# A gap of 192 bytes below the left-hand activation tiles of a diffusion block kernel

## Chip, cores and metric

One core of one Trainium2 chip runs the kernel. The metric is the device time of one execution in microseconds (us); the median of three runs before the change is 1629.53 us (1629.22 to 1630.85).

## What is computed

One block of a diffusion backbone over 256 latent tokens and 256 context tokens, width 2048, all in fp32. Cut to what matters:

```python
mod = silu(c) @ w_ada + b_ada                       # shifts, scales, gates for both sub-layers
h_lat, h_ctx = modulate(rmsnorm(x)), modulate(rmsnorm(ctx))
dq, dk, dv, cq, ckv, kr, ga, gb = split(h @ w_in)   # 8000 columns
o_da  = differential attention(dq, dk, dv)          # 8 heads
o_mla = latent attention(rmsnorm(cq) @ w_uq, rmsnorm(ckv) @ w_ukv, kr)
x = x + g1 * ((sigmoid(ga) * (rmsnorm(o_da) @ w_o_da) + sigmoid(gb) * (o_mla @ w_o_mla)) @ w_out)
h2 = modulate(rmsnorm(x))
x = x + g2 * ((silu(h2 @ w_ffn_gate) * (h2 @ w_ffn_up)) @ w_ffn_down)   # hidden width 5632
return rmsnorm(x)
```

## The kernel before

**Matrix products.** Each fp32 operand is held as a high part rounded to fp32r and a low part (the rest), and each product takes three matmuls: high x high, high x low, low x high. Weights arrive by 512 KB transfers from SyncE's queue into `raw` (five buffers, `load_w`), ScalarE rounds them into `wh` (three buffers, L140) and VectorE subtracts to make `wl` (three buffers, L141); the activation pairs (`hl`, `hc`, `oTa`, `oTb`, `cqn`, `ckvn`, `mT`, `h2`, `hid`) stay in SBUF. `group_t` computes 512 output columns for 256 tokens: the stationary operand is a 128x128 block of weights, the moving operand a 128x256 slice of the activations. One `group_t` over all 16 slices of the inner width is 8 units of 24 matmuls, 192 in all (over 8 slices, 4 units and 96). `group_b` turns it round: activations are stationary and the weights move (256 columns in `dv`, 512 in `down`). Each matmul has a weight load of its own, so every matmul reads one slice as moving operand while the next stationary block is being read. `Acc.mm` (L125, L127) issues them all.

**Stages.** Modulation and the first projections; four rounds of differential attention (`dk`, `dq`, `dv` from `hl`, `hc`); latent attention (`cq`, then `kn`, `mv`, `qn`, `qr` from `ckvn`, `cqn`); four rounds of `ga`, `gb` (from `hl`) and two `yab` (from `oTa`, `oTb`); `wo` (from `mT`); eleven rounds of `gate` and `up` (from `h2`, L889 to L901); four rounds of `down` (from `hid`). Beside them a generator (`gemv`, L452) streams parts of `w_ada` through the same `raw` buffers and sums them on VectorE (`gacc`, L461): a call of `tick` loads one 512 KB piece. In the FFN the `gate` rounds 3 to 6 have such a tick with each unit; `up` rounds have none. The order of TensorE's work is that of the program, and SyncE's queue issues the loads in program order as buffers come free.

**Where tiles lie.** Pools are two stacks in each partition's 224 KiB: `const`, `stream` (wl, wh, raw) and then all other pools opened without a side grow upwards from the left; pools with `side="right"` grow down from the top end. Every slice that a matmul reads starts a multiple of 512 bytes into its tile. The compiled program of before places them so (bytes within a partition):

| tiles | side | start | start mod 256 | mod 512 |
|---|---|---|---|---|
| wl, wh, three each | left | 25,120 to 45,600 in steps of 4,096 | 32 | 32 |
| ckvn (high, low) | left | 70,176 and 74,272 | 32 | 32 |
| h2 | left | 86,560 and 102,944 | 32 | 32 |
| oTa | left | 110,368 and 118,560 | 32 | 288 |
| oTb | left | 126,752 and 134,944 | 32 | 288 |
| cqn | left | 143,136 and 147,232 | 32 | 288 |
| hc, later mT | right | 163,808 and 180,192 | 224 | 480 |
| hl | right | 196,576 and 212,960 | 224 | 480 |
| hid | right | 130,528 and 175,584 | 224 | 480 |

In the differential attention the topmost left tile (`dvl`) ends at 163,616, and `hc` begins at 163,808.

Of the kernel before, what the change touches and what calls it, by code (L numbers as in the profile page):

```python
# [11 lines left out]
F32 = mybir.dt.float32  # L12
# [6 lines left out]
P = 128  # L19
# [49 lines left out]
def kernel(  # L69
# [11 lines left out]
    def pool(name, bufs=1, space=None, side=None):  # L81
        st = ExitStack()
        kw = {}
        if space is not None:
            kw["space"] = space
        if side is not None:
            kw["side"] = side
        pl = st.enter_context(tc.tile_pool(name=name, bufs=bufs, reuse_waits="tile", **kw))
        return pl, st.close
# [2 lines left out]
    ctx.callback(_c0)  # L92
    stream, _c1 = pool("stream")
    ctx.callback(_c1)
    pacc, _c2 = pool("pacc", space=PSUM)
    ctx.callback(_c2)

# [872 lines left out]
```

## Time and profile before

| | |
|---|---|
| median of three runs | 1629.53 us |
| profiled execution | 1625.1 us |
| its span, first to last instruction | 1623.3 us |
| TensorE busy | 1574.0 us (97%) |
| VectorE, ScalarE busy | 1018.1 us (63%), 736.6 us (45%) |
| read from HBM | 352.37 MB, 218 GB/s over the span |

The span is 1.8 us shorter than the profiled execution's own time. Busy time of TensorE counts each matmul from its start to a modelled end, and neighbours overlap; how fast matmuls follow one another is read from the length of an unbroken stretch divided by the matmuls in it. The views used are the page's tables, the chain of work that ended last, sums over windows of time, and groups by line.

### The profile page before, as it was taken

What the parts mean: (1) busy time and instruction counts of PE and PEld (TensorE: products, weight loads), DVE (VectorE), ACT (ScalarE), POOL (GpSimd) and SP (SyncE); (2) the same over time, 40 slices, a digit from 0 to 9 for tenths busy, and PEclk for the clock granted to TensorE, in tenths of its full rate; (3) what the DMA queues carried; (4) which work ended last, traced back from release to release, by engine and by line L of the source; (5) the groups of instructions that cost most, each with busy time, mean ns of one, the idle gap of its engine ahead of it and who ended that gap; (6) DMA issues with size and microseconds to landing.
All of it is one profiled execution on the core that took longest, in us unless ns stands there. A gap on an engine that the chain in (4) does not pass through costs nothing.

```text
span 1623.3 us, 28926 instructions
## 1 busy us (share of the span) xinstructions
PE 1574.0 (97%) x11936; PEld 1467.9 (90%) x11936; DVE 1018.1 (63%) x1356; ACT 736.6 (45%) x1033; POOL 16.1 (1%) x14
## 2 busy tenths in 40 slices
PE   4999999999999999899999999999999999999997
PEld 1778899999899999899999999999999999888886
DVE  6437888677875867677767476766444544444454
ACT  4325455546774434344346434444444344344343
POOL 0000000000000000000000000000000000011010
PEclk9999999999999999999999999999999999999999
DMA  9995754453347889888985677887666666656563
GB/s 330 353 354 170 220 157 144 130 170 101 96 130 235 296 285 305 278 282 279 309 275 169 187 265 263 267 279 246 184 184 185 185 184 199 201 191 189 193 194 117
DMA packets 197075, 356.35 MB, mean 220 GB/s; under 512 B 11984, under 2 KB 71632, under 8 KB 196688
## 3 DMA queue, kind: packets, MB, share of 16 engines
q1 hardware_dynamic: 196080, 351.58, 68.0%
q10 hardware_dynamic: 864, 2.93, 0.6%
q8 instruction: 93, 1.52, 0.4%
q14 instruction: 38, 0.31, 0.1%
HBM read 352.37 MB, written 2.10 MB: 218 GB/s over the span
## 4 chain that ended last, share of the span: by engine, by line
PE 75%; DMA 8%; DVE 4%; issue 1%; ACT 1%; DVEq 0%; POOLq 0%; POOL 0%; ACTq 0%; SPq 0%
PE gate L127 15%; PE up L127 15%; PE down L127 15%; DMA raw<-in_w_ada_dram 6%; PE dv L127 5%; PE yab L127 3%; PE ga L127 3%; PE gb L127 3%; PE dk L127 3%; PE wo L127 2%; PE dq L127 2%; DVE wl L141 1%; PE cq L127 1%; DVE gacc L461 1%; PE pt L601 1%
## 5 line engine op out<-in xcount | busy, mean ns | idle before, releaser
L141 DVE TENSOR_TENSOR wl<-raw,wh 128x1024 fp32r<-128x1024 f32 x452 | 550.3, 1223 | 375.5 <-ACT wh L140 352.7
L140 ACT CAST wh<-raw 128x1024 fp32r<-128x1024 f32 x452 | 474.2, 1050 | 628.3 <-PE down L127 137.1
L461 DVE SCALAR_TENSOR_TENSOR gacc<-raw,cols,gacc 128x1024 f32<-128x1024 f32 x120 | 153.9, 1283 | 97.3 <-DMA raw<-in_w_ada_dram 97.1
L127 PE MATMUL up<-h,wh 128*128 128x256 f32 x1386 | 183.8, 283 | 0.0
L127 PE MATMUL gate<-h,wh 128*128 128x256 f32 x1386 | 183.7, 283 | 0.0
L127 PEld LDWEIGHTS gate<-h,wh 128*128 128x128 f32 x1386 | 174.3, 192 | 0.4 <-DVE h L855 0.2
L127 PE MATMUL down<-wh,hid 128*128 128x512 f32 x696 | 174.5, 391 | 0.0
L127 PEld LDWEIGHTS up<-h,wh 128*128 128x128 f32 x1386 | 174.2, 192 | 0.0
L127 PEld LDWEIGHTS down<-wh,hid 128*128 128x128 f32 x696 | 130.8, 188 | 28.8
L127 PE MATMUL up<-h,wl 128*128 128x256 f32 x704 | 100.6, 283 | 0.0
L127 PE MATMUL gate<-h,wl 128*128 128x256 f32 x704 | 100.6, 283 | 0.0
L127 PE MATMUL down<-wl,hid 128*128 128x512 f32 x352 | 95.6, 392 | 0.0
L127 PEld LDWEIGHTS gate<-h,wl 128*128 128x128 f32 x704 | 91.6, 192 | 0.0
L127 PEld LDWEIGHTS up<-h,wl 128*128 128x128 f32 x704 | 91.6, 192 | 0.0
L127 PEld LDWEIGHTS down<-wl,hid 128*128 128x128 f32 x352 | 66.1, 188 | 14.1
L127 PE MATMUL ga<-hl,wh 128*128 128x256 f32 x504 | 65.4, 278 | 0.0
L127 PE MATMUL gb<-hl,wh 128*128 128x256 f32 x504 | 64.0, 277 | 0.0
L127 PE MATMUL wo<-mT,wh 128*128 128x256 f32 x504 | 63.7, 277 | 0.0
L127 PEld LDWEIGHTS ga<-hl,wh 128*128 128x128 f32 x504 | 61.1, 188 | 0.1
L127 PEld LDWEIGHTS gb<-hl,wh 128*128 128x128 f32 x504 | 60.6, 188 | 0.0
L127 PEld LDWEIGHTS wo<-mT,wh 128*128 128x128 f32 x504 | 60.1, 188 | 0.4 <-issue 0.4
L363 PE MATMUL pgb<-sraw,c 128*32 128x512 f32 x244 | 37.2, 607 | 20.5 <-DMA sraw<-in_w_ada_dram 20.5
(335 smaller groups left out, 2320.3 us busy)
## 6 DMA issues: line engine op xcount, KB each, us to landing
raw<-in_w_ada_dram SPq DMA_DIRECT2D x128, 512.0 KB, 4.7
raw<-in_w_in_dram SPq DMA_DIRECT2D x120, 512.0 KB, 4.8
raw<-in_w_ffn_gate_dram SPq DMA_DIRECT2D x88, 512.0 KB, 4.4
raw<-in_w_ffn_up_dram SPq DMA_DIRECT2D x88, 512.0 KB, 4.2
raw<-in_w_ffn_down_dram SPq DMA_DIRECT2D x88, 512.0 KB, 3.8
sraw<-in_w_ada_dram SPq DMA_DIRECT2D x122, 256.0 KB, 6.6
raw<-in_w_out_dram SPq DMA_DIRECT2D x32, 512.0 KB, 6.0
raw<-in_w_o_da_dram SPq DMA_DIRECT2D x16, 512.0 KB, 5.5
```

The lines of the kernel that those rows point to most:

```text
L127: nc.tensor.matmul(region, lhsT, rhs, start=False, stop=last, skip_group_check=key != self.lead)
L140: nc.scalar.copy(h, v)
L141: nc.vector.tensor_sub(l, v, h.bitcast(F32))
L363: nc.tensor.matmul(pgb[32 * j : 32 * j + 32, :], c32[:, kt, :], vs[kt], start=kt < 4, stop=kt >= 12, tile_position=(0, 32 * j))
L461: nc.vector.scalar_tensor_tensor(a, raw, cols[:, kt : kt + 1], a, op0=ALU.mult, op1=ALU.add)
L601: nc.tensor.transpose(pt[:, j * P : (j + 1) * P], a[:, j * P : (j + 1) * P], ident)
```

## The change

It opens one more pool on the left, after `stream` and before all the others, with one tile of 48 floats (192 bytes) per partition that nothing writes or reads. Every left-hand pool opened later starts 192 bytes higher; `const`, `stream` and the right-hand pools stay where they are. No instruction is added or taken away.

```diff
     stream, _c1 = pool("stream")
     ctx.callback(_c1)
+
+    apart, _c3 = pool("apart")
+    ctx.callback(_c3)
+    apart.tile([P, 48], F32, name="gap")
     pacc, _c2 = pool("pacc", space=PSUM)
     ctx.callback(_c2)
```

So `ckvn` and `h2` start at 224 mod 256 (224 mod 512), and `oTa`, `oTb` and `cqn` at 224 mod 256 (480 mod 512).

## Rows read from the trace of the kernel before

**Rows 1.** The page: busy time by engine, and the granted TensorE clock in 40 slices
```profile
PE 1574.0 (97%) x11936; PEld 1467.9 (90%) x11936; DVE 1018.1 (63%) x1356; ACT 736.6 (45%) x1033; POOL 16.1 (1%) x14
...
PEclk9999999999999999999999999999999999999999
```
**Rows 2.** The chain that ended last, four stretches: start us, us, what, matmuls
```profile
277.68 21.19 PE dv L127 x187
...
549.01 21.19 PE ga L127 x187
...
570.77 21.19 PE gb L127 x187
...
843.92 10.90 PE wo L127 x96
```
**Rows 3.** The same chain in the FFN
```profile
887.10 22.44 PE up L127 x187
...
910.14 22.44 PE gate L127 x187
...
1372.84 59.74 PE down L127 x261
...
1433.27 59.74 PE down L127 x261
```
**Rows 4.** The same chain in yab and in the latent attention
```profile
412.44 0.36 PE qr L127 x3
...
416.04 0.72 PE qn L127 x6
...
408.60 2.28 PE mv L127 x19
...
537.50 10.92 PE yab L127 x91
```
**Rows 5.** Windows of four groups: us, busy of PE PEld DVE ACT POOL, clock, DMA share, GB/s
```profile
549.01:570.77 21.76, 21.76 (x194) 21.76 (x194) 18.99 (x19) 10.89 (x12) 0.00 (x0) 1.00 0.91 306
...
887.10:910.14 23.04, 23.04 (x195) 23.04 (x194) 11.04 (x11) 9.87 (x11) 0.00 (x0) 1.00 0.66 194
...
1002.30:1026.25 23.95, 23.95 (x199) 23.79 (x198) 19.73 (x19) 11.39 (x13) 0.00 (x0) 1.00 0.87 297
1026.25:1049.29 23.04, 23.04 (x194) 23.04 (x194) 13.80 (x13) 8.43 (x11) 0.00 (x0) 1.00 0.76 241
```
**Rows 6.** Windows from the first yab to the end of wo, and its second yab alone
```profile
525.00:604.00 79.00, 79.00 (x685) 77.84 (x684) 56.45 (x53) 32.80 (x37) 0.00 (x0) 1.00 0.87 291
604.00:692.00 88.00, 82.42 (x688) 80.83 (x687) 64.71 (x64) 33.01 (x36) 0.00 (x0) 0.98 0.88 291
692.00:817.00 125.00, 119.49 (x1035) 117.95 (x1033) 90.31 (x91) 52.26 (x57) 0.53 (x1) 1.00 0.88 291
...
537.50:549.01 11.51, 11.51 (x99) 11.51 (x98) 8.93 (x9) 4.21 (x4) 0.00 (x0) 1.00 0.98 353
```
**Rows 7.** The chain between 610 and 817 us, the first and last of its loads
```profile
610.19 5.11 DMA raw<-in_w_in_dram
...
808.56 4.74 DMA raw<-in_w_ada_dram
```
**Rows 8.** Groups by line: line engine op names shapes xcount | busy us, mean ns | idle before
```profile
L601 PE MATMUL pt<-cols,t 128*128 128x128 f32 x128 | 19.9, 275 | 0.0
...
L374 PE MATMUL pgb<-cols,res 128*128 128x128 f32 x32 | 4.9, 275 | 0.7 <-ACT res L372 0.7
```

## The prediction

> **What bounds the kernel now.** I read the page's first tables, then the chain of work that ended last, then windows of time around single groups of matmuls. The page shows TensorE busy for 97% of the span at full clock (2.4 GHz) in all 40 slices [rows 1], so the question is how densely its matmuls follow one another. A busy share cannot tell that, because a matmul's recorded time overlaps its neighbour's. An unbroken piece of the chain can: divide its length by its matmuls. Do that for pieces with the same shape, 128x128 stationary and 128x256 moving. `dv`, `ga` and `gb` give 21.19/187 = 113.3 ns, `wo` 10.90/96 = 113.5 ns [rows 2]. `gate` and `up` give 22.44/187 = 120.0 ns [rows 3], `yab` 10.92/91 = 120.0, `qn` and `qr` 0.72/6 and 0.36/3 = 120.0, `mv` 2.28/19 = 120.0 [rows 4]. There are two speeds and nothing between them. Records missing from a trace can't make this: a whole group of 192 takes 21.76 us for `ga` and 23.04 us for `up` from start to start [rows 5], which is 113.3 and 120.0 ns again.
>
> What separates the two speeds? Not the routine: `ga`, `wo`, `gate` and `yab` all come from `group_t`, with the same order of matmuls. Not the clock, which is 1.00 in both windows, and not the loads: the fast `ga` window moves 306 GB/s and the slow `up` window 194 [rows 5]. Not which operand is the activation: it is stationary in `dv` (fast) and `mv` (slow), moving in the others. What does separate them is the table of positions. In every fast group the activations begin at 224 mod 256 and the weights at 32; in every slow one both begin at 32 mod 256. Every slice starts a multiple of 512 bytes into its tile, so this holds for each matmul of a group. `h2` and `oTa` differ by 256 bytes mod 512 and cost the same 120.0 ns, so a step of 256 seems not to matter.
>
> **The change part by part.** It adds no instruction, no transfer and no written wait. It moves `h2`, `oTa`, `oTb`, `ckvn` and `cqn` from 32 to 224 mod 256 while the weights stay at 32. That is the pair of positions of all the fast groups, so I take 113.3 ns for the moved ones.
>
> Gate and up: 22 groups, each 23.04 - 21.76 = 1.28 us shorter [rows 5], is 28.2 us for their 4224 matmuls. All of it is on the path: the chain of the FFN is `gate` and `up` matmuls, one after the other [rows 3]. What is late next there? VectorE is busy 11.04 us of an `up` group and at most 19.73 of a gate group with `w_ada` loads [rows 5]; the latter would be 21.76 + 0.91 us long, 0.91 being the 23.95 - 23.04 of the extra matmuls that gate group already holds. So VectorE stays below the new length.
>
> yab: 4 rounds of 2 groups of 96 are 768 matmuls, at 6.67 ns 5.1 us. Three of the eight groups lie before 604 us, where TensorE doesn't wait, the others in a stretch whose chain hops from load to load [rows 7]. But the rate of the loads is 291 GB/s before 604 us as after it, with the DMA engines 0.87 and 0.88 busy [rows 6]; the second `yab` alone has 0.98 and 353 GB/s. Faster matmuls there would only wait more before 817 us. Ends: 0 to 5.1 us; I take 0, by the loads.
>
> Latent attention: per pair of heads 24 `mv` and 36 `qn` and `qr` matmuls, four pairs, 240 at 6.67 ns: 1.6 us. They come before the loads bind. Ends 0 and 1.6; I take 1.5, since these pieces stand on the chain themselves [rows 4]. `kn` (512 wide) has no fast counterpart with the same operands; left at 0.
>
> What stays: `down` (right-hand `hid`, weights not moved) at 59.74/261 = 228.9 ns [rows 3]; `dq`, `dk`, `dv`, `cq`, `ga`, `gb`, `wo`. Scores and value products of both attentions have both operands on the left; they move together. The transposes read a left tile `t` against the constant identity; with a right-hand tile `res` at 224 mod 256 they take the same 275 ns mean [rows 8], so 0.
>
> Two costs that no row shows. VectorE and ScalarE may work at another speed on moved tiles: in the FFN VectorE idles half of an `up` group [rows 5], so a few per cent either way are hidden there. And the moved tiles lie on slightly other remains of freed right-hand tiles, so some first write may wait for another release: from 0 to about one wait for a load, 5.11 us [rows 7]. The topmost, `dvl`, now ends exactly where `hc` begins, without overlap. I take 0 for both.
>
> Sum: 28.2 + 0 + 1.5 = 29.7 us. The profiled execution, 1625.1 us with a span of 1623.3, comes to 1595.4. The median of the runs is 4.4 us above that execution; taken from it, 1629.5 - 29.7 = 1599.8 us. With both ends of `yab` and latent attention the saving is 28.2 to 34.9 us, that is 1594.6 to 1601.3; with a microsecond of scatter (the three runs span 1.6) 1593.5 to 1602.
>
> A rule speaks against this. The Trainium skill, "TensorE: Matmul & The Clock Gate", section "Step-by-step: what each phase is for", says: "Loading the next tile's weights doesn't steal SBUF read bandwidth from the running matmul", the two reads having a port each. By that rule no position could matter and the time would be the first rival's, 1629.5 us. The rows above disagree with it: 113.3 against 120.0 ns with nothing else different that I can find.
>
> **The rivals.** First, no change, 1629.5 us: the position mod 256 is only a mark of something else. In every slow group both operands lie on the left, below byte 151,328, and in every fast one the activations lie at 163,808 or above, so it could be the region of the memory that costs, and 192 bytes change no region. Against it: `hid` begins at byte 130,528, inside the region of the slow tiles, and `down` runs its blocks at one speed [rows 3]; but `down` is 512 wide, so this is weak. The tile that nothing uses might also get no room at all. The point to decide it is the spacing in `gate`: 120.0 again.
>
> Second, the loads take part of it back. A gate group with `w_ada` pieces needs 16 loads of 512 KB, 8.39 MB; at the highest rate seen, 353 GB/s [rows 6], that is 23.8 us, longer than the new 21.76. If nothing were loaded ahead, four groups would lose 2.0 us each, 8.0 in all: 1607.8 us. For it: the window of such a group already runs at 297 GB/s and 0.87. Against it: gate and up together need 12.58 MB in 43.5 us, 289 GB/s, the five `raw` buffers and three `wh`/`wl` pairs carry work ahead, and the `up` group takes up the rest.
>
> Third, half of it: the new positions are between the two speeds, 116.7 ns, saving about 15 us: 1614.7. No row shows such a speed.
>
> Fourth, slower: the pattern repeats after 512 bytes, not 256. Then `h2` at 224 mod 512 is at a position that no fast group has (they are at 480), and could read worse than now. The same step the other way, 6.67 ns more, on 4224 matmuls costs 28.2 us; with 1.5 us gained elsewhere the time is 1656.2. It decides the sign once gate's spacing passes 120.0 + 1.5/4224, about 120.4 ns. For it: no row shows 224 mod 512 on the left. Against it: the equal cost of `h2` (32 mod 512) and `oTa` (288).
>
> **How the numbers follow.** Forecast 0.77, no change 0.10, loads 0.06, half 0.02, slower 0.05. The likeliest is 1599.8 us. The range 1593 to 1610 holds the forecast with its bounds and the second rival, about 0.82, leaving out no change, half and slower. Its sign is not in doubt within the range. Faster by over 0.2% (3.3 us, about what a measurement of this kernel can tell from no change): 0.77 + 0.06 + 0.02 = 0.85. Same: 0.10. Slower: 0.05.
>
> **What would show it.** In the profile after, a chain piece of 187 `gate` or `up` matmuls takes 21.2 us instead of 22.44, and groups start 21.76 us apart; `yab` pieces of 91 take 10.3 us, `qn` pieces of 6 take 0.68. `ga`, `dv`, `wo` and `down` keep their spacing. The load-bound stretch still ends near 817 us, one or two us earlier. Wrong would be: gate at 120.0 (first rival), TensorE waiting for `wl` in gate rounds 3 to 6 (second), a gate spacing between (third) or above 120.4 ns (fourth), or a span that falls by the right sum out of other stages.

## The result and the profile after

The changed kernel took 1603.58 us (median of four, 1599.34 to 1607.71) against 1629.38 before: ratio 0.9849, 95% interval 0.9819 to 0.9878. A second series gave 1609.15 (seven runs, 1601.94 to 1611.42) against 1628.47: 0.9885 (0.9866 to 0.9904). Both medians lie in the predicted range; the slowest run of the second series, 1611.42, lies beyond it. The working instructions of every engine stand in the same order in both compiled programs. Besides the addresses only a few waits of VectorE and ScalarE differ, and the program after has two more instructions that do nothing but wait. The profiled execution took 1607.2 us, its span is 1605.4, 17.9 shorter than before.

The page after, busy time and granted clock, against [rows 1]:

```profile
PE 1553.0 (97%) x11936; PEld 1444.4 (90%) x11936; DVE 1016.8 (63%) x1356; ACT 736.0 (46%) x1033; POOL 16.1 (1%) x14
...
PEclk9999999999999999999999999999999999999999
```

The chain that ended last, after (start us, us, what, matmuls), against [rows 3, 4]:

```profile
414.89 0.68 PE qn L131 x6
...
526.61 2.24 PE yab L131 x19
...
890.11 22.02 PE up L131 x187
...
912.73 22.02 PE gate L131 x187
...
1026.62 21.19 PE up L131 x187
...
1048.38 21.19 PE gate L131 x187
...
1354.93 59.74 PE down L131 x261
```

The 120.0 ns are gone from `gate`, `up`, `yab` (2.24/19 = 117.9 in this piece) and `qn` (0.68/6 = 113.3). From 1026 us on the forecast spacing stands, 21.19/187 = 113.3 ns. But between 877 and 1022 us the same matmuls follow one another at 22.02/187 = 117.8 ns. `down` is as before. That second spacing was not new. The chain of the kernel before has it in the `gb` group one round ahead of that of [rows 2] (and in a piece of `dv`), and I passed over it:

```profile
502.40 22.02 PE gb L127 x187
```

It isn't the clock. Two windows of equal length after, one in each stretch (us, busy of PE PEld DVE ACT POOL, clock, DMA share, GB/s), hold 1148 and 1194 matmul records at clock 1.00. The loads differ between them; a second profile, further down, has the fast spacing beside the denser loads.

```profile
880.00:1015.00 135.00, 135.00 (x1148) 135.00 (x1148) 82.97 (x77) 58.06 (x61) 0.00 (x0) 1.00 0.78 249
1130.00:1265.00 135.00, 135.00 (x1194) 135.00 (x1193) 67.45 (x62) 59.13 (x62) 0.00 (x0) 1.00 0.66 193
```

What TensorE's weight loads waited for in `gate` and `up`, after, besides 0.2 us for `h2` that they waited for before too (waiting line, releaser: us in total, times, longest):

```profile
PEld gs L887 <- DVE wl L145: 0.9, 1, 0.9
PEld gate L131 <- DVE wl L145: 0.4, 1, 0.4
```

The wait of `gate` is near 877 us, where the spacing changes from 113.3 to 117.8; that of `gs` (the matmuls of `keep`, fed by `w_ada`) is near 1111 us.

Where the 17.9 us came from. `up` of the first round to the first unbroken piece of `down` took 1372.84 - 887.10 = 485.7 us and takes 1354.93 - 890.11 = 464.8: 20.9 less, for 21 groups that by the prediction bring 26.9. The six groups at 117.8 cost 6 x 0.85 = 5.1 of the difference, and the wait for `keep`'s weights 0.9. Ahead of that, `up` starts 3.0 us later than before (890.11 against 887.10), though `qn` and `yab` are faster.

### The profile page after: what moved, and what is told of

Its sections match the earlier page's. It is cut to its first block, busy times and chain, and to the rows that moved or that the text cites. A ratio compares the mean times of both kernels' runs of the same rounds, so it can differ in the third digit from the quotient of the medians.

```text
span 1605.4 us, 28928 instructions
## 1 busy us (share of the span) xinstructions
PE 1553.0 (97%) x11936; PEld 1444.4 (90%) x11936; DVE 1016.8 (63%) x1356; ACT 736.0 (46%) x1033; POOL 16.1 (1%) x14
## 4 chain that ended last, share of the span: by engine, by line
PE 67%; DMA 11%; DVE 7%; issue 2%; ACT 2%; DVEq 0%; POOLq 0%; ACTq 0%; POOL 0%; SPq 0%
PE down L131 15%; PE up L131 14%; PE gate L131 13%; DMA raw<-in_w_ada_dram 8%; PE dv L131 5%; PE wo L131 3%; PE dk L131 3%; DVE wl L145 3%; PE dq L131 2%; DVE gacc L465 2%; PE gb L131 1%; PE ga L131 1%; PE cq L131 1%; DMA raw<-in_w_in_dram 1%; DMA raw<-in_w_o_mla_dram 1%
## 5 line engine op out<-in xcount | busy, mean ns | idle before, releaser
L131 PE MATMUL gate<-h,wh 128*128 128x256 f32 x1386 | 176.4, 278 | 0.0
L131 PE MATMUL up<-h,wh 128*128 128x256 f32 x1386 | 176.1, 277 | 0.0
L131 PEld LDWEIGHTS gate<-h,wh 128*128 128x128 f32 x1386 | 167.2, 188 | 0.4 <-DVE h L859 0.2
L131 PEld LDWEIGHTS up<-h,wh 128*128 128x128 f32 x1386 | 166.8, 188 | 0.0
L131 PE MATMUL gate<-h,wl 128*128 128x256 f32 x704 | 97.0, 278 | 0.2 <-DVE wl L145 0.2
L131 PE MATMUL up<-h,wl 128*128 128x256 f32 x704 | 96.8, 277 | 0.0
L131 PE MATMUL down<-wl,hid 128*128 128x512 f32 x352 | 95.6, 392 | 0.0
L131 PEld LDWEIGHTS gate<-h,wl 128*128 128x128 f32 x704 | 88.0, 188 | 0.4 <-DVE wl L145 0.4
L131 PEld LDWEIGHTS up<-h,wl 128*128 128x128 f32 x704 | 87.9, 188 | 0.0
```

Source lines behind the costliest of these rows:

```text
L131: nc.tensor.matmul(region, lhsT, rhs, start=False, stop=last, skip_group_check=key != self.lead)
```

## The experiments

Two theories stood against each other. One: what counts is the distance between the addresses of the two operands, mod 256 bytes, and each unbroken stretch of matmuls keeps one of the spacings that its distance allows. The other: the place of the activations, or waits and loads, make the difference.

**The FFN alone.** The gap stands below `h2`, and not below the earlier left-hand tiles.

```diff
+    fgap, close_fg = pool("fgap")
+    fgap.tile([P, 48], F32, name="fgap")
     xtp, close_xt = pool("xtp")
```

> The 192 bytes stand only below the FFN's left tiles, so h2 alone goes to 224 mod 256; yab, mv, qn and qr stay as before. Theory (relative position of the two operands that TensorE reads): gate and up at 113.3 ns in an undisturbed stretch, at 117.8 ns after some waits, as in the changed kernel; yab stays at 120.0. Time 1629.4 less 20 to 28, so 1601 to 1609 us. Rival (the saving comes from all the left tiles or from waits that went): gate and up keep 120.0 or the time falls by clearly less than 20 us.

Measured: 1604.93 us, ratio 0.986 (0.9838 to 0.9882), the same as the whole change. Its chain, with a profiled execution of 1598.21 us:

```profile
536.13 10.92 PE yab L127 x91
...
885.22 21.19 PE up L127 x187
...
1345.95 59.74 PE down L127 x261
```

`yab` has its 120.0 back and the time doesn't mind; `gate` and `up` alone carry the gain. Here they ran at 113.3 from the first `up` on: 1345.95 - 885.22 = 460.7 us, 25.0 less than before. The missing 1.9 of 26.9 are waits of `keep`:

```profile
PEld gs L885 <- DVE wl L141: 1.8, 2, 1.1
PEld gate L127 <- DVE wl L141: 0.4, 1, 0.4
```

The wait of `gate` at the fifth unit is there too, and the stretch behind it took 113.3. The same wait ended in either spacing.

**256 bytes instead of 192** (the tile above with 64 floats).

> The gap below the FFN's left tiles is 256 bytes: h2 at 32 mod 256 and 288 mod 512. Theory (the pattern repeats after 256 bytes): gate and up back at 120.0 ns, time as before, 1628 to 1631 us. Rival (a pattern of 512 bytes or more, or any shift away from the old place helps): gate and up at another spacing, 113 to 118 ns, and some 20 us less.

Measured: 1627.1 us in one run, and 120.0 ns:

```profile
889.09 22.44 PE up L127 x187
...
912.13 22.44 PE gate L127 x187
```

So not any shift helps, and a shift of 256 bytes counts as none.

**Weights and left activations together** (the change's pool opened ahead of `stream`, so wl, wh, raw move too).

```diff
+    apart, _c3 = pool("apart")
+    ctx.callback(_c3)
+    apart.tile([P, 48], F32, name="gap")
     stream, _c1 = pool("stream")
```

> The 192 bytes stand below the weight tiles, so weights and left activations both move to 224 mod 256; the right-hand activations stay at 224. Left activations lie where the changed kernel has them, but their distance to the weights is 0 again, and that of the right-hand ones becomes 0 too. Theory (only the distance counts): gate, up and yab at 120.0 ns, and ga, gb, wo, dv, dq, dk rise from 113.3 to 120.0 too; down rises by 0 to 4 ns. Sum on the path: 1536 matmuls of dq, dk and dv, 192 of cq, some 1100 of ga, gb and wo outside the load-bound stretch, at up to 6.7 ns, and 1056 of down at up to 3.6: 12 to 23 us more than before, 1641 to 1653 us. Rival (the place of the activations alone counts, or the region): gate and up at 113 to 118 and 1600 to 1608 us, or no change at all.

Measured: 1637.41 us, ratio 1.0058 (1.0038 to 1.0078), slower, though less than expected. Its chain:

```profile
282.84 22.44 PE dv L130 x187
...
558.95 22.44 PE ga L130 x187
...
859.45 11.51 PE wo L130 x96
...
903.23 22.44 PE up L130 x187
...
1388.99 59.17 PE down L130 x261
```

`h2` lies exactly where the change puts it and pays 120.0 ns; `hl`, `hc` and `mT` have not moved and pay 120.0 too [rows 2]. Only the distance to the weights can tell these apart from the kernels above. (The run moved `raw` with `wl` and `wh`; TensorE reads the latter two alone.) One expectation was wrong in sign: `down`, 512 wide, is faster at distance 0, 59.17/261 = 226.7 ns against 228.9.

**Other distances.** Three kernels with other gaps below the left-hand tiles, a second one below `oTb`, and a third below `h2`.

```diff
-    apart.tile([P, 48], F32, name="gap")
+    apart.tile([P, 32], F32, name="gap")      # 128 bytes; 32 and 96 in the other two
...
+    ogap.tile([P, 48], F32, name="ogap")      # below oTb: 192; 128 and 128
...
+    fgap.tile([P, 8], F32, name="fgap")       # below h2: none; 32 and 64
```

> Other distances from the weights: h2 and oTa 128 bytes on (160 mod 256), oTb, cqn and kn 64 bytes on (96 mod 256). Theory (a cost that depends on the distance): gate, up and the yab of oTa share one spacing, the yab of oTb and qn another; 192 has 113.3 or 117.8, and 64 is its mirror image, so 113.3 or 117.8 there too; 128, the farthest, at most that, and perhaps without the slow state. Time at 113.3 throughout: 1600 us or less. Rival (192 is the one good distance): gate at 120.0, 1627 to 1631 us.

> Three more distances: oTa 32 bytes on (the yab of oTa), oTb, cqn and kn 160, h2 64. Theory (cost by distance mod 256, with a few steady spacings): the 64 of h2 gives 113.3 or 117.8, as the yab of oTb did at 64; 32 lies nearer to 0 and gives 117 to 120; 160 lies between 128 (118.6 or 120) and 192 (113.3 or 117.8). Time 1600 to 1615 us. Rival (only the exact distance 192 is good): gate and up at 120, 1627 us.

> The rest of the distances: oTa 96, oTb, cqn and kn 224, h2 160. Theory (cost by distance mod 256): gate and up between those of 128 and 192, 113 to 119 ns; 96 like 160, 224 like 32. If any distance has 113.3 without the second spacing, or less than 113.3, it is the better place. Time 1600 to 1627 us. Rival (only 192): gate and up at 120, 1627 us.

Measured: 1623.23 us (ratio 0.997, 0.9953 to 0.9987); 1616.62 and 1619.43, one run each. The chains, first with `h2` at distance 128 (`yab` of `oTb` at 64), then 64 (`oTb` at 160), then 160 (`oTb` at 224):

```profile
606.46 10.73 PE yab L130 x91
...
890.38 22.19 PE up L130 x187
...
1028.05 22.44 PE up L130 x187
```
```profile
537.19 10.68 PE yab L130 x91
...
887.53 22.02 PE up L130 x187
```
```profile
680.76 10.77 PE yab L130 x91
...
886.57 22.19 PE up L130 x187
```

| distance of the moving activations from the weights, mod 256 | spacing seen in gate and up |
|---|---|
| 0 (before; 256; all moved) | 120.0 ns |
| 64 | 117.8 |
| 128 | 118.7, and 120.0 after the matmuls of keep |
| 160 | 118.7 (117.4 in the `yab` piece above) |
| 192 | 113.3 or 117.8 |

The mirror image that I expected isn't there: at 64 no unbroken piece of `gate`, `up` or `yab` had 113.3, while at 192 many had. Yet in `dv`, where the weights move and lie 64 on from the stationary `hl`, 113.3 is common [rows 2], so the distance alone doesn't settle it; which operand moves, or how the stretch began, comes in too, and that stays open. 32, 96 and 224 were tried in `yab` alone, without 113.3 in the pieces read; 224 has 10.77/91 = 118.4 above, and the longest unbroken piece at 32 had 116.9. For a moving activation 192 is the only distance tried that showed 113.3.

**The changed kernel again.**

> The changed kernel once more, to see its scatter. Theory (an unbroken stretch of matmuls keeps one of two spacings, 113.3 or 117.8 ns, drawn when it starts; gate and up from 877 to 1023 us are one such stretch): the times fall into two clusters some 6 us apart, near 1599 and 1606, and the profile belongs to the cluster that its spacing in that stretch says: 113.3 with a span near 1597, 117.8 with one near 1605. Rival (the lost microseconds come from load waits in the FFN): one broad cluster, and the gate spacing of the profile does not go with its time.

Measured: 1601.94 to 1611.42 us, not two clean clusters but a spread. The profile belongs to the fastest execution, and its FFN stretch has 113.3 throughout, with more loaded in the window that was slow above (249 GB/s there, 261 here), so the loads don't make the slow spacing:

```profile
888.93 21.19 PE up L131 x187
...
1349.73 59.74 PE down L131 x261
...
880.00:1015.00 135.00, 135.00 (x1193) 135.00 (x1193) 86.38 (x79) 58.94 (x63) 0.00 (x0) 1.00 0.79 261
```

1349.73 - 888.93 = 460.8 us, 4.0 less than in the first profile, as six groups at 0.85 less and 1.0 more waiting of `gs` give. Between these two profiles the spacing goes with the time, and the other 1.2 us of difference lie ahead of the FFN. The executions without a profile, up to 1611.42 us, can't be divided so.

**A break between gate and up.** A transpose that nothing reads, in each round of the changed kernel.

```diff
+        with tc.issue_after(recent[0].ins):
+            nc.tensor.transpose(ps_x(nm("brk"))[:, :P], ident, ident)
         bk = group_t(w_up, c0, 512, KT, [act_t(h2)], "up")
```

> The changed kernel with one 128x128 transpose of the identity, read by nothing, between the gate and the up matmuls of each round: 11 more matmuls of about 0.11 us. Theory (a break draws the spacing anew): the spacing can change at these breaks and only at breaks, so no stretch of 117.8 is longer than two groups, and the times come closer together, between 1599 and 1606 plus 1.2 us; if a break by an fp32 matmul leads to 113.3 nearly always, as after pgb and gs, then all near 1600. Rival (the spacing is that of a whole execution, or of a stage, and not drawn at breaks): two clusters as without the transposes, 1.2 us later.

Measured: 1616.88 us (1615.68 to 1618.63), ratio 0.9931 (0.9914 to 0.9948). Close together, as the theory has it, but higher:

```profile
911.62 22.03 PE gate L132 x187
934.36 21.19 PE up L132 x187
956.12 21.24 PE gate L132 x187
978.05 22.02 PE up L132 x187
```

Spacing changes at a break and is kept over the next `gate`, where nothing breaks the stream (the pieces are `up`, then `gate`). Of the eleven stretches behind a transpose three had 113.3 and eight 117.8; my guess that such a break mostly leads to 113.3 was wrong.

**A 512-wide break**, in place of the transposes: `h2[0][:, 0, :P]` stationary and the last `wh` moving, after the `gate` matmuls of each round.

> As the kernel with transposes between gate and up, but the extra matmul is 512 columns wide (a block of h2 stationary, the last wh moving, into a bank that nothing reads), after the gate matmuls of each round: 11 more matmuls of 0.23 us, 2.5 us. After the four 512-wide matmuls of keep the spacing was 113.3 every time so far, after a transpose mostly 117.8. Theory (what comes before a stretch sets its spacing, and a 512-wide matmul sets 113.3): every gate and up stretch after the first extra matmul at 113.3, all runs together near 1600 + 2.5, 1600 to 1605 us. Rival (each break is a lottery whatever it is): stretches of both spacings, 1606 to 1612 us.

Measured: 1627.37 us, ratio 0.9994 (0.9985 to 1.0003): the whole gain is gone.

```profile
894.02 22.02 PE up L132 x187
...
1373.07 60.90 PE down L132 x261
```

All stretches behind these matmuls had 117.8, and `down`, which followed the last one unbroken, 60.90/261 = 233.3 ns against 228.9. Against a stream at 113.3 throughout, 21 groups lose 17.9 us, the 1056 matmuls of `down` 4.7, and the extra matmuls take the expected 2.5: the 25 us of the gain. Not a lottery, then, and not what I had set out for either.

**No wait at the head of the FFN.** Four of the `ht` products leave VectorE.

```diff
+        if kt > 7 and kt % 2:
+            nc.scalar.mul(t, x2T[:, kt, :], gs2[:, kt : kt + 1])
+            nc.gpsimd.tensor_mul(t, t, y)
+        else:
```

> The changed kernel with four of the sixteen ht products at the head of the FFN made by ScalarE and GpSimd, so that VectorE reaches the fifth wl some 1.6 us sooner and TensorE should not wait 0.2 to 0.4 us for it near 877 us. Theory (that wait is where the slow spacing of gate rounds 1 to 4 is drawn; the stretch before it had 113.3 each time): no wait there, 113.3 from the start of gate to the keep matmuls, one cluster of times, 1597 to 1603 us. Rival (the spacing of the stretch doesn't hang on the wait): 117.8 from some point in about half of the runs, and times to 1608 us.

Measured: 1600.66 to 1610.38 us, ratio 0.9852 (0.983 to 0.9874). The wait of `gate` for `wl` is gone, and the profiled execution, the slowest of its five, has 117.8 from the first group on (its 192 matmuls, two of them without a record, take 22.64/192 = 117.9):

```profile
869.32 22.64 PE gate L131 x190
892.56 22.02 PE up L131 x187
...
1029.23 21.19 PE up L131 x187
```

So the wait isn't what makes the slow stretch: the start of the stream can do it as well. This theory fell.

**Both gains together**: one 512-wide break in the first round only, and `hid` 192 bytes lower, at distance 0 from the weights.

> The changed kernel with one 512-wide extra matmul after the gate matmuls of the first round only, and hid moved down by 192 bytes, to 32 mod 256, the place of the weights (ones_r stays). In the kernel that moved everything left, down ran at distance 0 from the weights and took 239.2 us from its first to its last matmul, not 241.5. Theory (both gains add): gate and up at 113.3 from the second group on, down 2.3 us shorter, 0.2 us for the extra matmul; 1596 to 1603 us in one cluster. Rival (512-wide matmuls at distance 0 only looked faster because of the other order of things there): down at 241.5 us; or the first stretch after the extra matmul at 117.8 in some runs, 6 us more.

Measured: 1603.82 us (1600.53 to 1604.71), ratio 0.9845 (0.9832 to 0.9858). `down` is 59.16/261 = 226.7 ns, as expected, and the stretch from 888 us had 117.8:

```profile
888.85 22.02 PE up L132 x187
...
1025.48 21.19 PE up L132 x187
...
1354.82 59.16 PE down L132 x261
```

**Four matmuls as keep issues them**, `ones_r` stationary, in place of the one; `hid` as in the last kernel.

> As the kernel with hid at 32 mod 256, but with four 512-wide matmuls of the kind that keep issues (ones_r stationary; the high and the low part of the last weights moving), after the gate matmuls of the first round. After keep's own four the spacing was 113.3 in all fourteen places seen, after one 512-wide matmul with a block of h2 it was 117.8 in all. Theory (what was issued just before a stretch sets its spacing): up and gate at 113.3 from about 889 us to the keep matmuls, down 2.3 us shorter, 0.9 us for the four matmuls, times together at 1595 to 1601 us. Rival (keep's stretches owe their spacing to the idle time or the waits around it, not to the matmuls): 117.8 in that stretch, 1601 to 1606 us.

Measured: 1606.62 us (1605.71 to 1607.75), ratio 0.9862 (0.9846 to 0.9879). The piece of `gate` before the four had 113.5 ns from start to start (12.08/104 = 116.2 with the pause at its head and missing records), the `up` behind them 117.8:

```profile
876.72 12.08 PE gate L132 x104
...
890.29 22.02 PE up L132 x187
```

The rival holds: it isn't the matmuls of `keep` that lead to 113.3. What does, in all the stretches behind `keep`'s own four, stays open. No version here is faster than the change beyond its interval.

## Why the prediction was right, and where not

**The mechanism and the main term.** That gate and up leave 120.0 ns because the distance to the weights becomes 192 mod 256 is shown: 256 bytes bring 120.0 back, moving the weights along brings it back with `h2` in its new place, and moving `h2` alone gives the whole gain. The 28.2 us were too many. For the 21 groups from the first `up` on, the sum had 26.9; 25.0 came where the stretch ran at 113.3, and 20.9 where part of it ran at 117.8. The step that failed is "there are two speeds and nothing between them": the chain of before held a third, in the `gb` group at 502.40 us, and I had divided only the group of the next round. That both medians still lie in the range is in part luck: it reached to 1610 for the loads, and the second spacing took up that room.

**What is late next.** "VectorE stays below the new length" held as an average and failed at single places: TensorE waits 0.4 us for the fifth `wl` at the head of the FFN and 0.9 to 1.9 us in `keep`. The waits in `keep` are the second rival, the loads, at a quarter of its 8.0 us or less: the chain to the one at 1111 us runs from a `w_ada` load of 5.62 us that landed at 1107.3 through `gacc`, `wh` and `wl`. The 0.4 us are VectorE's own, which makes the last parts of `h2` there without a pause.

**yab at 0.** Right: with `yab` at 120.0 in the kernel with the gap in the FFN alone the median is the same. The stretch with `yab` in it took no less time: from the first long piece of `ga` (487.44 us before) to the last of `wo` (843.92) it is 356.5 us before, 358.2 and 359.5 in the two profiles of the change. That it would end one or two us earlier, as forecast, did not happen.

**Latent attention at 1.5.** Mis-sized and not seen in the sum. `qn` fell to 113.3 ns, but from the last long piece of `cq` to the first of `ga` the stretch takes 95.2 us in both profiles of the change, 95.9 before, and 95.6 and 95.5 in the kernels with the gap below `h2` only: some 0.5 us gained. `up` of the first round even starts 1.8 to 3.0 us later than before, and 1.9 earlier in the kernel with 192 bytes below `h2` only. For the first profile of the change a good part of the delay can be seen: by 219 us it is 2.4 us late. TensorE had stood still for 2.6 us ahead of the scores of the attention (2.1 us before), and then the granted clock was 0.50, that is 1.2 GHz, where before it was 1.00 (the same window after and before):

```profile
194.00:197.00 3.00, 2.78 (x11) 2.59 (x12) 2.91 (x7) 2.69 (x7) 0.00 (x0) 0.50 0.61 176
...
194.00:197.00 3.00, 3.00 (x24) 2.83 (x23) 3.00 (x6) 2.66 (x7) 0.00 (x0) 1.00 0.59 159
```

The page's 40 slices show 9 throughout in both, so "full clock in all 40 slices" was too coarse a reading. Eight of the eleven profiles of kernels with a gap below all the left-hand activations have this fall, and none of the other three; whether the moved tiles bring it about is not shown. The second profile of the change doesn't have it: its delay arises in the load-bound stretch, which scatters by as much without moved tiles (355.3 us with 192 bytes below `h2` only, 358.4 with 256).

**down unchanged.** Right for the change. That it would gain by distance 0 was not foreseen.

**The rivals.** No change (region): refuted by the change itself, which left `h2` in its region, and by the kernel that moved the weights, where activations of the upper region pay 120.0. Slower (a pattern of 512 bytes): refuted by the change too, since `h2` at 224 mod 512 became faster; and with the 256-byte gap 288 mod 512 costs what 32 costs. Half: there is a speed between, 117.8, at a third of the way from 120.0 to 113.3; at one and the same distance a stretch has either it or 113.3. The rule of the Trainium skill that loading the next weights steals no SBUF read bandwidth from the running matmul ("TensorE: Matmul & The Clock Gate", "Step-by-step: what each phase is for") would leave no room for a position to matter. The measurement decides against it here: with the same matmuls in the same order, 113.3 to 120.0 ns by the distance of the two operands. Why the distance counts inside the chip is not shown.

## What to carry to other kernels

When a group of matmuls has a spacing that others of the same shape don't have, compare the addresses of its two operands before its schedule; here 192 spare bytes in the right place were worth over 1% of the time, and the wrong 192 bytes cost 0.6%. Divide unbroken pieces of the chain by their matmuls for every group, not for a sample, since one that runs between two known speeds says that the better one isn't assured. A faster stage gains only where it is the bound, and it finds the waits that its slowness covered.

## What the runs showed of the hardware

- Spacing of 256-wide fp32r matmuls at full clock depends on how far the moving operand starts above the stationary one, mod 256 bytes. With activations moving it was 120.0 ns at 0, 117.8 at 64, 118.7 or 120.0 at 128, 118.7 at 160, 113.3 or 117.8 at 192; with weights moving, in `dv`, 113.3 or 117.8 at 64. For 512-wide ones it is 226.7 at 0 and 228.9 or 233.3 with the stationary operand 192 further on.
- At one distance the stream can hold one of two spacings over more than 1200 matmuls and changes it only at a break: a wait of 0.4 us, or a matmul of another kind. Which one it takes behind a break was always 117.8 after one or four inserted 512-wide matmuls (13 stretches), mixed after transposes and after the wait, and always 113.3 behind `keep` (16 places, with `h2` at 192); why is not settled.
